# Who makes the high half of the softmax probabilities: one helper's choice of engine

## The chip, the cores and the metric

The kernel runs on one core of one Trainium2 chip. The metric is the device time of one execution in microseconds (us); a comparison of versions goes by the median of several executions. PE is the matrix engine, ACT the scalar engine, DVE the vector engine, POOL is GpSimd, and SP is the engine whose queue issues most of the DMAs.

## The reference

One layer of a hybrid encoder on a sequence of 2048 positions with 1024 features, in float32. Cut to what matters here:

```python
u    = rms_norm(h, norm1_w)
proj = einsum('bsd,de->bse', u, w_in)            # dq | dk | dv | sq | sk | sv
# differential attention: 4 heads, two softmax maps per head, value width 128
logits = einsum('bqhcd,bkhcd->bhcqk', qb, k) * scale + bias   # dq, dk are normed before
logits = where(mask, logits, -inf)               # chunk-causal, chunks of 64
p      = softmax(logits, axis=-1)
attn   = p[:, :, 0] - lam * p[:, :, 1]           # the probabilities of this case
y_diff = einsum('bhqk,bkhd->bqhd', attn, v)
# stick-breaking attention: 8 heads of width 64, no softmax, strictly causal
h = h + concat(norm(y_diff), norm(y_sb)) @ w_out
h = h + SwiGLU(rms_norm(h))                      # width 2816
```

## The kernel before

All large products run on PE in float16 with each operand split in two: a high part (the value cast to float16) and a low part (the value minus its high part, cast to float16). Three products (high by high, high by low, low by high) then stand for one in float32. So each tile of attention probabilities has to be split before PE can use it.

**Stages.** The input projection is cut into eight groups `g`. Groups 0 to 3 hold one softmax head each (function `diff_attn`), groups 4 to 7 two stick-breaking heads each (`sb_attn`). The loop at the end of the first phase goes through the groups; while the heads of group g are worked on, the generator `proj_stream` gives out the projection tiles of the next group, so the two kinds of work share all engines. The output projection and the feed-forward stage follow.

**A softmax head** goes over 16 blocks `i` of 128 queries. `probs(i)` makes the scores of both maps on PE, brings them into tiles `z` with their maxima on DVE (lines 542 and 546), takes the exponentials on ACT in place (line 556), and joins the two maps into one on DVE: `z0 = z1 * rc + z0` (line 566, both inputs in SBUF). Block i reaches over (i+1)*128 keys, in tiles of at most 1024: one tile for i below 8, two from there on. That gives 96 tiles in the four heads, 40 of them with 1024 elements in each partition. Each goes through `split_t` (line 449): a cast into the front of a buffer `s16` by `to16`, a subtraction into its back by `tt` (line 98), and a DMA transpose issued by SP (line 460) into a tile `aT`. There are three `s16` buffers. `values(i)` multiplies `aT` with the values `v` on PE (line 517, in `pv`); it is called two blocks behind `probs`. The tiles' names in the profile are cut: `s` stands for `s16`.

**The choice of engine.** `to16` and `tt` ask `pick` for an engine: the one with the least running sum after its own cost. The sums (`load`) are kept while the program is written, not on the chip; `note` adds work that has a fixed engine; `level` sets them to zero at every fourth block.

```python
def to16(dst, src, n, engines="ADP", psum=False):
    cost = {"A": 0.84 * n + 110, "D": (1.05 if psum else 0.53) * n + 70, "P": 1.1 * n + 80}
    e = pick(**{k: cost[k] for k in engines})
# tt: cost = {"D": 1.15 * n + 70, "P": 2.45 * n + 80}, engines="DP"
def split_t(src, n, he="ADP", le="DP", wide=None):
    ...
    to16(s16[:, :n], src, n, he)
    tt(s16[:, n : 2 * n], src, s16[:, :n], ALU.subtract, n, le)
    ...
    SP.dma_start_transpose(aT[:, : 2 * n // P, :], s16[:, : 2 * n])
```

`to16` writes a cast as an ACT copy (line 89), a DVE copy (line 91) or a POOL instruction (line 93). The stick-breaking heads call `split_t` with ACT for the cast and POOL for the subtraction already.

The same two helpers serve the batches of queries and keys of the groups below 4 (`proj_batch`, line 386, once for every four projection tiles): one multiplication of `raw` by `gk` with `tt` (line 402), then twice a cast of 512 elements from `raw` into `st` (line 406) and its subtraction (line 407). ACT also empties the projection's PSUM tiles `pj` (lines 360 and 374); there are two of them.

**The order** of the instructions on each engine is set by the framework's scheduler, which simulates the program; within an engine they start in that order. The attention work has a raised priority.

Of the kernel before, what the change touches and what calls it, by code (L numbers as in the profile page):

```python
# [59 lines left out]
def block(tc, a, out):  # L60
# [3 lines left out]
    with top:  # L64
# [8 lines left out]
        def note(e, ns):  # L73
            load[e] += ns * KW[e]
# [10 lines left out]
# [3 lines that stand above are left out]
            if e == "A":  # L88
                ACT.copy(dst, src)  # L89
            elif e == "D":  # L90
                DVE.tensor_copy(dst, src)
            else:
                POOL.tensor_scalar(dst, src, 1.0, 0.0, op0=ALU.mult, op1=ALU.add)

        def tt(dst, a_, b_, op, n, engines="DP"):
            cost = {"D": 1.15 * n + 70, "P": 2.45 * n + 80}
            e = pick(**{k: cost[k] for k in engines})
            (DVE if e == "D" else POOL).tensor_tensor(dst, a_, b_, op)  # L98

        def pri(k):  # L100
            def deco(f):
                @functools.wraps(f)
                def g(*args):
                    with tc.high_priority(PRI[k]) if PRI[k] else nullcontext():
                        return f(*args)
                return g
            return deco

        def nm(s):
            uid[0] += 1  # L110
            return f"{s}{uid[0]}"
# [144 lines left out]
        with ExitStack() as ph1:  # L256
# [6 lines left out]
            def z4():  # L263
                return zp.tile([P, 1028], F32, tag="z4", bufs=ZB, name=nm("z4"))
# [183 lines left out]
            @pri("spl")  # L448
            def split_t(src, n, he="ADP", le="DP", wide=None):
                if wide is not None and wide % 5 in (1, 3):  # L450
                    s16 = pp.tile([P, 4, 256], F32, tag="raw", name=nm("s16"))[:].rearrange("p t n -> p (t n)").bitcast(F16)
                else:
                    s16 = s16p.tile([P, 2048], F16, tag="s16", bufs=SB, name=nm("s16"))
                to16(s16[:, :n], src, n, he)
                tt(s16[:, n : 2 * n], src, s16[:, :n], ALU.subtract, n, le)
                if wide is not None and wide % 4 == 3:
                    aT = pp.tile([P, 4, 4, 2, 64], F16, tag="st", name=nm("aT"))[:].rearrange("p c t s e -> p (c t) (s e)")
                else:
                    aT = sp.tile([P, 16, P], F16, tag="aT", bufs=AB, name=nm("aT"))
                SP.dma_start_transpose(aT[:, : 2 * n // P, :], s16[:, : 2 * n])  # L460
                return aT
# [40 lines left out]
            @pri("sc")  # L502
            def score_chunk(G, sc, i, q, m, w, cut=False, turned=False):
                terms = ((m, 0), (2 + m, 0), (m, 1)) if turned else ((2 + m, m), (m, m))
                for o, (a_, b_) in enumerate(terms):
                    last = PE.matmul(sc[:, : 128 * w].rearrange("p (t n) -> p t n", n=P), lhsT=G["q"][i // 4][:, a_, i % 4, :], rhs=G["k"][q][:, b_, 0:w, :], start=o == 0, stop=o == len(terms) - 1)  # L506
                if cut:
                    last = PE.matmul(sc[:, 128 * w - P : 128 * w], lhsT=idb[:], rhs=tri[:], start=False, stop=True, skip_group_check=True)
                return last.ins
# [9 lines left out]
            def diff_attn(g, G):  # L519
                @pri("at")  # L520
                def probs(i):
                    L = (i + 1) * 128
                    near = max(0, i - 1) * 128
                    nb = i // 8 + 1
                    zs = [[], []]
                    if i % 4 == 0:
                        sums[0] = sm.tile([P, 4, 2], F32, tag="sums", bufs=3, name=nm("sums"))
                    su = sums[0][:, i % 4, :]
                    mx = sm.tile([P, 2, 8], F32, tag="mx", name=nm("mx"))
                    for m in range(2):  # L530
                        nx = 0
                        for b in range(nb):
                            n = min(1024, L - 1024 * b)
                            z = z4()
                            for c in range((n + 511) // 512):
                                lo, hi = 512 * c, min(512 * c + 512, n)
                                sc = ps.tile([P, 512], F32, tag="sc", bufs=4, name=nm("sc"))
                                score_chunk(G, sc, i, 2 * b + c, m, (hi - lo) // P)
                                f = min(max(near - 1024 * b - lo, 0), hi - lo)
                                note("D", 1.05 * (hi - lo) + 200)  # L540
                                if f > 0:
                                    DVE.tensor_scalar(z[:, lo : lo + f], sc[:, :f], kz_d[:], None, op0=ALU.mult, op1=ALU.max, accum_out=mx[:, m, nx : nx + 1])
                                    nx += 1
                                if f < hi - lo:
                                    b0 = 1024 * b + lo + f - (i - 1) * 128
                                    DVE.tensor_tensor_reduce(z[:, lo + f : hi], sc[:, f : hi - lo], bias[:, g, b0 : b0 + hi - lo - f], kz_d[:], -3.0e38, ALU.add, ALU.max, mx[:, m, nx : nx + 1])
                                    nx += 1
                            zs[m].append((b, n, z))
                    ng = sm.tile([P, 2], F32, tag="ng", name=nm("ng"))
                    if nx > 1:  # L550
                        DVE.tensor_reduce(ng[:], mx[:, :, :nx], op=ALU.max, axis=AX.X)
                    ACT.activation(ng[:], ng[:] if nx > 1 else mx[:, :, 0], AF.Identity, bias=lnc[:], scale=-1.0)
                    s2 = sm.tile([P, 2, 2], F32, tag="s2", name=nm("s2")) if nb > 1 else None
                    for m in range(2):
                        for b, n, z in zs[m]:
                            ACT.activation(z[:, :n], z[:, :n], AF.Exp, bias=ng[:, m : m + 1], accum_out=(s2[:, m, b : b + 1] if nb > 1 else su[:, m : m + 1]))
                            note("A", 0.84 * n + 300)
                    if nb > 1:
                        DVE.tensor_reduce(su, s2[:], op=ALU.add, axis=AX.X)
                    rc = sm.tile([P, 1], F32, tag="rc", name=nm("rc"))  # L560
                    DVE.reciprocal(rc[:], su[:, 1:2])
                    DVE.tensor_scalar(rc[:], rc[:], mlam[:], su[:, 0:1], op0=ALU.mult, op1=ALU.mult)
                    note("D", 600)
                    aTs = []
                    for (b, n, z0), (_, _, z1) in zip(*zs):
                        DVE.scalar_tensor_tensor(z0[:, :n], z1[:, :n], rc[:], z0[:, :n], op0=ALU.mult, op1=ALU.add)
                        note("D", 1.05 * n + 130)
                        aTs.append((b, n, split_t(z0[:, :n], n)))
                    return aTs

                sums = {}
# [13 lines left out]
                for i in range(NT):  # L585
                    if i % 4 == 0:
                        level()
                    held.append((i, probs(i), sums[0]))
                    if len(held) > 2:
                        values(*held.pop(0))  # L590
                    yield ((i + 1) * (i + 2) / 2 + CD * (i + 1)) / (136 + 16 * CD), i + 1
# [706 lines left out]
```

## Time and profile before

| What | us |
|---|---|
| median of three executions | 2706.24 (2704.32 to 2712.25) |
| the profiled execution | 2704.82 |
| its span, first to last instruction | 2702.7 |
| PE busy in the span | 2500.8 |
| DVE busy | 1956.5 |
| POOL busy | 1516.4 |
| ACT busy | 1346.4 |

The span is what the views of the profile divide up; the time of the execution is 2.1 us more. Busy time is the sum of an engine's instructions; the waits are listed apart, each with the instruction that ended it.

### The profile page before, as it was taken

The page shows a single profiled execution, that of the slowest core. Times are in us where ns is not written, and L with a number is a line of the kernel's source. Part 1 is how long each engine was busy: PE and PEld are TensorE (multiplying, and loading weights), DVE is VectorE, ACT ScalarE, POOL GpSimd, SP SyncE. Part 2 cuts the span into 40 slices and gives each one's busy share as a digit, 9 for nine tenths or more (in the row PEclk, how much of TensorE's full clock was granted, in tenths as well). Part 3 has the DMA queues.
Part 4 walks back from the last instruction along what each step waited for, and adds up shares of the span by engine and source line. Part 5 has one row for each costly group of instructions (what it writes and reads, how often), then busy time and mean ns, then how long its engine had stood idle before and what let it go on. Part 6 is the DMA issues. An engine that isn't in the chain of part 4 may idle for free. (4 is left out here: it accounts for less than half of the span.)

```text
span 2702.7 us, 50511 instructions
## 1 busy us (share of the span) xinstructions
PE 2500.8 (93%) x19628; PEld 1502.5 (56%) x19628; DVE 1956.5 (72%) x3711; ACT 1346.4 (50%) x2488; POOL 1516.4 (56%) x1097
## 2 busy tenths in 40 slices
PE   7998989898988989889998999999999999999999
PEld 4655556577776776567784444444444444444444
DVE  6888879899989989877856777778685543433434
ACT  4665656567978878665735534345352112111121
POOL 2577767767767767546655565565564332322322
PEclk9999999999999999999999999999999999999999
DMA  7777687769989989987995566565749744635532
GB/s 230 201 166 180 143 200 173 178 151 178 196 176 185 178 169 209 206 200 211 222 335 204 210 236 220 198 234 190 253 171 338 293 158 160 234 132 184 201 111 94
DMA packets 619584, 534.40 MB, mean 198 GB/s; under 512 B 480640, under 2 KB 548224, under 8 KB 609104
## 3 DMA queue, kind: packets, MB, share of 16 engines
q1 hardware_dynamic: 617520, 529.09, 69.8%
q8 instruction: 154, 2.52, 0.4%
q0 software_dynamic: 512, 1.36, 0.2%
q10 hardware_dynamic: 1312, 0.72, 0.1%
q14 instruction: 86, 0.70, 0.1%
HBM read 261.08 MB, written 147.32 MB: 151 GB/s over the span
## 5 line engine op out<-in xcount | busy, mean ns | idle before, releaser
L98 POOL TENSOR_TENSOR s<-z,s 128x1024 f16<-128x1024 f32 (+7 forms) x288 | 471.9, 1648 | 140.9 <-ACT s L89 116.3
L506 PE MATMUL sc<-kT,qT 128*128 128x512 f16 (+3 forms) x1520 | 381.6, 353 | 53.5 <-DVE z L622 19.0
L1104 PE MATMUL pd<-wd,act 128*128 128x512 f16 x1764 | 391.8, 379 | 8.1 <-DVE cu L1038 7.1
L621 DVE TENSOR_TENSOR_SCAN z<-z,sc 128x512 f32<-128x512 f32 (+3 forms) x320 | 352.8, 1112 | 56.7 <-ACT sc L619 34.9
L325 PE MATMUL pj<-w,xt 128*128 128x384 f16 x1920 | 353.1, 332 | 17.2 <-ACT raw L374 5.9
L1004 PEld LDWEIGHTS <-wg 128*128 128x128 f16 x1848 | 181.5, 98 | 226.1 <-issue 12.4
L1004 PEld LDWEIGHTS <-wu 128*128 128x128 f16 x1848 | 181.5, 98 | 220.2 <-issue 7.1
L517 PE MATMUL yp<-v,aT 128*128 128x64 f16 (+1 forms) x4896 | 269.1, 204 | 37.3 <-DMA aT<-s 36.2
L517 PEld LDWEIGHTS <-aT 128*128 128x128 f16 x4896 | 236.9, 99 | 115.4 <-DMA aT<-s 47.7
L98 POOL TENSOR_TENSOR act<-cg,act 128x512 f16<-128x512 f32 x109 | 150.6, 1392 | 262.5 <-ACT act L1063 262.5
L1104 PEld LDWEIGHTS <-act 128*128 128x128 f16 x1764 | 172.6, 98 | 216.6 <-issue 10.1
L325 PEld LDWEIGHTS <-xt 128*128 128x128 f16 x1920 | 187.5, 99 | 146.9 <-issue 23.3
L89 ACT CAST s<-z 128x128 f16<-128x128 f32 (+7 forms) x215 | 173.1, 810 | 135.8 <-DMA aT<-s 41.0
L98 POOL TENSOR_TENSOR stages<-stages 128x512 f32<-128x512 f32 x97 | 171.6, 1769 | 119.1 <-DVE wg L220 41.3
L618 ACT ACTIVATE z<-sc,c 128x512 f32<-128x512 f32 (+3 forms) x320 | 210.6, 663 | 25.1 <-PE sc L506 12.5
L98 POOL TENSOR_TENSOR hs<-hs,cu 128x512 f32<-128x512 f32 x102 | 132.5, 1307 | 158.1 <-DVE hs L1110 58.0
L506 PEld LDWEIGHTS <-qT 128*128 128x128 f16 x1520 | 128.2, 99 | 121.4 <-issue 23.5
L1063 ACT CAST act<-cg 128x512 f16<-128x512 f32 x126 | 76.8, 616 | 237.5 <-DVE cg L1069 199.4
L831 PE MATMUL po<-wo,mt 128*128 128x256 f16 x1536 | 182.5, 279 | 12.2 <-DVE xf L834 8.4
L1110 DVE SCALAR_TENSOR_TENSOR hs<-pd,c,hs 128x512 f32<-128x512 f32 x144 | 106.5, 748 | 116.3 <-PE pd L1104 112.2
L341 PE MATMUL pj<-xt,w 128*128 128x128 f16 x2304 | 176.9, 222 | 6.2 <-DVE v L363 5.2
L1004 PE MATMUL pm<-X,wu 128*128 128x512 f16 x792 | 179.3, 379 | 1.8 <-ACT cg L1049 1.7
(255 smaller groups left out, 4803.5 us busy)
## 6 DMA issues: line engine op xcount, KB each, us to landing
xt<-xs SPq DMA_DIRECT2D x112, 512.0 KB, 4.3
hs<-hd SPq DMA_DIRECT2D x72, 512.0 KB, 4.4
hd<-hs SPq DMA_DIRECT2D x56, 512.0 KB, 5.4
split<-wg SPq DMA_DIRECT2D x11, 1792.0 KB, 6.9
split<-wu SPq DMA_DIRECT2D x11, 1792.0 KB, 6.7
split<-wd SPq DMA_DIRECT2D x11, 1792.0 KB, 6.8
wg<-split SPq DMA_DIRECT2D x11, 1792.0 KB, 7.3
wd<-split SPq DMA_DIRECT2D x11, 1792.0 KB, 8.7
```

What stands on the lines that cost most here:

```text
L89: ACT.copy(dst, src)
L98: (DVE if e == "D" else POOL).tensor_tensor(dst, a_, b_, op)
L325: PE.matmul(pj[:, :384], lhsT=xv[:, xi, kt, :], rhs=G["w"][:, wi, kt, :], start=n == 0, stop=n == 23)
L341: PE.matmul(o, lhsT=x_ if c == 2 else w_, rhs=w_ if c == 2 else x_, start=n == 0, stop=n == 23)
L506: last = PE.matmul(sc[:, : 128 * w].rearrange("p (t n) -> p t n", n=P), lhsT=G["q"][i // 4][:, a_, i % 4, :], rhs=G["k"][q][:, b_, 0:w, :] ...
L517: PE.matmul(yp[:, y0 : y0 + wd], lhsT=aT[:, a_, :], rhs=v[:, v_ : v_ + wd], start=start and j == 0 and q == 0, stop=stop and j == nb - 1 a ...
L618: ACT.activation(om[:, lo:hi], sc[:, :w], AF.Sigmoid, scale=G["nkz"][:])
L621: DVE.tensor_tensor_scan(ov, ov, sc[:, :w], om[:, hi : hi + 1], op0=ALU.mult, op1=ALU.bypass)
L831: PE.matmul(po[:, sl], lhsT=mt[:, kt, P * xi : P * xi + P], rhs=wos[2 * h + n][wi][:, kt, :], start=q == 0, stop=q == 23)
L1004: PE.matmul(ps_[:].rearrange("p (t n) -> p t n", n=P), lhsT=wv[:, wo, wi, 128 * kt : 128 * kt + 128], rhs=X[xo][:, :, xi, kt, :], start=st ...
L1104: PE.matmul(po[:], lhsT=act[:, ao, xi, 128 * j : 128 * j + 128], rhs=W["d"][:, wo, wi, :], start=start and u == 0 and q == 0, stop=u == nu ...
L1110: DVE.scalar_tensor_tensor(dst, po[:], kd[:], src, op0=ALU.mult, op1=ALU.add)
```

## The change

In `diff_attn` the call of `split_t` gets "A" as its third argument, so that the cast of the probabilities is always an ACT instruction. The subtraction is chosen as before among DVE and POOL. The costs still enter the running sums.

```diff
@@ -565,7 +565,7 @@
                     for (b, n, z0), (_, _, z1) in zip(*zs):
                         DVE.scalar_tensor_tensor(z0[:, :n], z1[:, :n], rc[:], z0[:, :n], op0=ALU.mult, op1=ALU.add)
                         note("D", 1.05 * n + 130)
-                        aTs.append((b, n, split_t(z0[:, :n], n)))
+                        aTs.append((b, n, split_t(z0[:, :n], n, "A")))
                     return aTs
```

## The prediction

> **What bounds the kernel now.** I read the page first, then the busy time by window, then the waits of PE, then the groups of the stage that the change touches.
>
> ```profile
> span 2702.7 us, 50511 instructions
> PE 2500.8 (93%) x19628; PEld 1502.5 (56%) x19628; DVE 1956.5 (72%) x3711; ACT 1346.4 (50%) x2488; POOL 1516.4 (56%) x1097
> 110.00:615.00 505.00, 458.18 (x4029) 308.31 (x4028) 440.25 (x1306) 311.08 (x801) 360.28 (x257) 0.98 0.74 170
> ```
>
> The last row is the window from 110 to 615 us, in which the 96 tiles of the softmax heads are joined (line 566). Its columns after the length are the busy times of PE, weight loads, DVE, ACT and POOL. PE is busy 458.2 of 505 us, DVE 440.3, POOL 360.3, ACT 311.1. So PE stands still for 46.8 us; that is all that any change of this stage can win there, 1.7% of the span. What PE waits for in the same window:
>
> ```profile
> PE yp L517 <- DMA aT<-s: 23.5, 16, 2.9
> PE pj L325 <- ACT raw L374: 5.9, 3, 3.4
> PE sc L506 <- DVE z L542: 3.7, 7, 1.5
> ```
>
> Columns: total us, number, longest. Half of PE's idle time is the wait for transposed probabilities, which is the end of the chain join (566), cast, subtraction, transpose. The cast is a link of this chain. The second row matters for the price: ACT also empties the projection's PSUM tiles, and PE stops when it is late with that.
>
> **The part that moves.** The groups of this window, by line:
>
> ```profile
> L98 POOL TENSOR_TENSOR s<-z,s 128x1024 f16<-128x1024 f32 (+6 forms) x95 | 160.0, 1694 | 12.8 <-ACT s L89 9.9
> L93 POOL TENSOR_SCALAR s<-z 128x1024 f16<-128x1024 f32 (+7 forms) x72 | 78.8, 1099 | 95.3 <-DVE z L566 93.6 <-DMA aT<-s 1.8
> L89 ACT CAST st<-raw 128x512 f16<-128x512 f32 x27 | 16.6, 614 | 27.0 <-POOL raw L98 12.7 <-DVE raw L399 12.2 <-DVE ng L551 2.0
> L89 ACT CAST s<-z 128x128 f16<-128x128 f32 (+6 forms) x24 | 15.3, 636 | 34.6 <-DMA aT<-s 16.6 <-DVE z L566 12.0 <-DVE mx L546 3.7
> ...
> L93 POOL TENSOR_SCALAR s<-z x73: 301/1047/2014, 111.3 to 617.3; 128x1024 f16<-128x1024 f32 x37, 128x640 f16<-128x640 f32 x8, 128x384 f16<-128x384 f32 x7, 128x896 f16<-128x896 f32 x5
> L93 POOL TENSOR_SCALAR st<-raw x1: 617/617/617, 68.1 to 68.1; 128x512 f16<-128x512 f32 x1
> ```
>
> Of the 96 casts POOL does 73 and ACT 23 (the 24th ACT cast of the window is of a stick-breaking head); DVE does none. All subtractions are on POOL. The change therefore moves 73 casts from POOL to ACT. Their price on each side:
>
> ```profile
> L93 POOL TENSOR_SCALAR s<-z 128x1024 f16<-128x1024 f32 x37 | 50.6, 1368 | 66.3 <-DVE z L566 66.3
> L89 ACT CAST s<-z 128x1024 f16<-128x1024 f32 x3 | 3.1, 1045 | 5.5 <-DVE z L566 5.5
> L89 ACT CAST s<-z 128x512 f16<-128x512 f32 x4 | 2.5, 614 | 11.1 <-DMA aT<-s 11.1
> ```
>
> *POOL loses* 78.8 us of work, and with it the 93.6 us that it stood waiting for the join in front of these casts. *ACT gains* 37 times 1.045 us, 38.7 us, and the 36 smaller ones: the two ACT rows give 0.842 ns an element and 0.183 us for each instruction; 8 of 640, 7 of 384, 5 of 896 and 16 others (four each of 768, 512, 256 and 128, what is left of the eight tiles of each size) are 18,944 elements, so 16.0 + 6.6 = 22.6 us. Together 61.3 us.
>
> *A second move hides in the running sums.* Every cast that goes to ACT raises ACT's sum and leaves POOL's lower, and the next choice reads these sums. Followed through the listing, they give for the program before 23 ACT and 73 POOL casts, as the trace has. At the third query/key batch of a group, for example, they stand at ACT 11,374 and POOL 13,789 before (POOL already with the multiplication by `gk`), so the 512-element cast goes to ACT (11,374 + 540 against 13,789 + 643). With the change they are 14,609 and 9,808, and it goes to POOL. This turns round in all 12 batches of groups 1 to 3: 24 casts `st<-raw` go from ACT to POOL, at 0.617 us by the one such row of POOL, 14.8 us. All subtractions stay on POOL, and all evictions of `pj` stay on ACT, since DVE's sum is the largest throughout.
>
> Net in the window: ACT 311.1 + 61.3 - 14.7 (24 times 0.614) = 357.7 of 505 us, 71%; POOL 360.3 - 78.8 + 14.8 = 296.3 us, 59%. Neither becomes the fullest engine. None of this is on the path by itself; what counts is whether `aT` comes sooner and what ACT delays.
>
> **What the chain gains: an ordinary block.** From the timeline, block 12 of the third head, with two tiles:
>
> ```profile
> 453.04 2.35 DVE L566 SCALAR_TENSOR_TENSOR z<-z,rc,z 128x1024 f32<-128x1024 f32 x2
> 454.57 1.13 ACT L556 ACTIVATE z<-z,ng 128x1024 f32<-128x1024 f32 x1
> 454.68 2.30 POOL L93 TENSOR_SCALAR s<-z 128x1024 f16<-128x1024 f32 x2 [1.17 <-DVE z L566]
> 455.71 0.92 ACT L556 ACTIVATE z<-z,ng 128x768 f32<-128x768 f32 x1
> 456.95 3.48 POOL L98 TENSOR_TENSOR s<-z,s 128x1024 f16<-128x1024 f32 x2
> 459.11 2.89 SPq L460 DMA_TRANSPOSE aT<-s  x2
> 459.87 2.58 DVE L566 SCALAR_TENSOR_TENSOR z<-z,rc,z 128x1024 f32<-128x1024 f32 x2
> ```
>
> POOL does both casts (2.30 us), then both subtractions. On ACT the first cast would end at 454.68 + 1.05 = 455.73, and POOL could start its subtraction then instead of at 456.95: 1.2 us sooner. But at 454.68 ACT is in the exponentials of the next block, which end at 456.63. If the scheduler puts the cast behind them, it ends at 457.68, 0.7 us later than now. So one block lies between 1.2 us gained and 0.7 us lost. I take 0.5 us gained, nearer to the gain, since ACT is free for 38% of the window even before anything is relieved.
>
> The 1024-element cast took 1.368 us on POOL, beside DVE's second join, and 1.045 us on ACT: 37 x 0.32 = 12 us that POOL loses beside DVE and ACT does not. I count them as POOL's time only, as they stand in the 78.8 us already. The Trainium skill, "SBUF — State Buffer", section "Who interferes with whom", has a rule for this: DVE and GpSimd share a pair of ports, an instruction of DVE with two SBUF inputs takes it against a GpSimd instruction that reads SBUF, the second to come waits in full, and ACT never waits. The trace agrees with the part on ACT; were the joins as often the blocked side, DVE would get up to the same 12 us back by that rule, which would be the last rival below.
>
> **What the chain gains: the change of heads.** At 350 to 375 us (and likewise near 220 and 490) POOL is behind:
>
> ```profile
> 358.25 1.64 POOL L93 TENSOR_SCALAR s<-z 128x128 f16<-128x128 f32 x2
> 359.88 3.50 POOL L219 TENSOR_SCALAR w<-wst,sW 128x1536 f16<-128x1536 f32 x2
> 363.35 2.00 POOL L93 TENSOR_SCALAR s<-z 128x384 f16<-128x384 f32 x1
> 365.32 2.55 POOL L98 TENSOR_TENSOR s<-z,s 128x128 f16<-128x128 f32 x2
> 367.27 2.48 SPq L460 DMA_TRANSPOSE aT<-s  x2
> 369.12 0.62 ACT L89 CAST st<-raw 128x512 f16<-128x512 f32 x1 [6.37 <-POOL raw L98]
> 369.60 0.34 PE L517 MATMUL yp<-v,aT 128*128 128x128 f16 x3 [2.67 <-DMA aT<-s]
> ```
>
> Casts of 1.64 and 2.00 us stand in POOL's queue ahead of the subtractions for which PE then waits 2.67 us, while ACT stands idle for 6.37 us behind a cast of `raw` that needs POOL. With the change the 3.6 us leave POOL's queue, and the cast that held ACT goes to POOL. Here I take the whole wait away: 2.67 us, at three changes of heads some 5 us beyond the ordinary 0.5 each (between 0, if the order there is unkind, and 8).
>
> **Sum.** Sixteen waits for `aT`: 16 x 0.5 = 8 us, less than the 23.5 they have; the changes of heads bring it to 13 at best. Against it: 61 us more ACT work, of which some delays an eviction. The row is 5.9 us of PE waiting for ACT in 505 us; in proportion to ACT's idle time (193.9 us before, 147.3 after) it would be 7.8, so 2 us, and the same again for the exponentials that come later and so the joins of the next block: 4 us. A PE that waits less for `aT` also meets the next late thing, scores whose `z` DVE has not yet emptied (3.7 us now, 440 of 505 us of DVE work); I give back 4 of the 13 to that. 13 - 4 - 4 = 5 us. The profiled execution, 2704.82 us, becomes 2699.8; the median of the runs lies 1.4 us above it, so I predict 2701 us, between 2688 (waits gone) and 2705. A measurement of this kernel can tell about 0.3%, 8.1 us, from no change.
>
> **The rivals.**
>
> *ACT is held up in order (slower).* A cast can't start before its `s16` buffer is free, that is before a transpose has landed. On POOL such a wait holds only other casts and subtractions. On ACT it holds the exponentials and the evictions.
>
> ```profile
> 236.33 9.52 SPq L460 DMA_TRANSPOSE aT<-s  x4
> 243.43 0.45 POOL L93 TENSOR_SCALAR s<-z 128x256 f16<-128x256 f32 x1 [1.08 <-DMA aT<-s]
> 245.34 0.51 POOL L93 TENSOR_SCALAR s<-z 128x384 f16<-128x384 f32 x1 [0.70 <-DMA aT<-s]
> ```
>
> At the change of heads the transposes went out from 236.33 in 9.52 us, and POOL's next casts waited for them. ACT's 24 casts already wait 16.6 us for `aT`, 0.69 us each, and 34.6 us in all. With 72 more at 1.44 us, ACT stands 104 us longer, of the 147 that it has left. It decides once ACT waits for a buffer while both `pj` tiles are full; three changes of heads at half of the 9.52 us each (two `pj` tiles cover the other half), 14 us, and the 16 waits for `aT` at the 0.7 us lost above, 11 us, less the 8 us that the rest still gains, make 17 us: 2723. For it speaks the 16.6 us; against it that the joins follow each other on DVE (453.04 and 459.87 above, 6.8 us apart), and in between ACT has nothing to take up but what DVE gives it, so that such a wait often costs nothing.
>
> *Nothing comes of it.* PE and DVE are the full engines and neither loses an instruction; if the time freed before `aT` turns into waits for scores, the sum is 0 to 2 us: 2705. By the Trainium skill, "Perfetto Trace Analysis", section "Identifying the Most-Contended Engine", one works on the engine with the highest occupancy first, which is neither POOL nor ACT. By that rule alone the result would be this one; the trace is half with it, for 23.3 of PE's 46.8 idle us aren't waits for `aT`.
>
> *It wins more.* All 23.5 us of waits go, and only 4 come back: 2685 to 2688. It needs the cast ahead of the exponentials in nearly every block.
>
> That the change does not do what it says I leave at nothing: the argument is passed on as it stands.
>
> **How the numbers follow.** Small gain, 0.40; held up in order, 0.30; nothing, 0.15; more, 0.15. Faster by over 8.1 us: the last case, and nearly half of the first (its range to 2688 passes 2698), 0.15 + 0.19 = 0.34. Slower: the second case, 0.30. Within: the rest, 0.36. The range reaches from the large gain to past the middle of the slow case, 2684 to 2728.
>
> **What would show it.** Right: in the window ACT near 358 us and POOL near 296 of some 500; 24 casts `st<-raw` at line 93; the subtraction's row with ACT as what ended its waits; PE's wait for `aT` under 16 us; ACT's wait for POOL's `raw` gone. Wrong to the slow side: "PE pj L325 <- ACT raw L374" above 15 us, "ACT s L89 <- DMA aT<-s" above 60. Wrong altogether: a changed time behind 615 us, where no instruction is another one and only the order could have moved.

## The result and the profile after

The changed kernel is slower, by little but clear of the noise: 2724.57 us median of 6 runs (2719.45 to 2731.82), the kernel before 2708.12 (2703.47 to 2712.25) beside it. The ratio is 1.0058 [1.0041, 1.0074], about 16 us. The forecast was 2701; to a clearly slower kernel it gave a chance of 0.30. The profiled execution took 2725.54 us, its span 2723.4.

The page after, its first lines, and the window of the softmax stage (columns after the length: PE, weight loads, DVE, ACT, POOL, granted clock, DMA share, GB/s):

```profile
span 2723.4 us, 50531 instructions
PE 2509.9 (92%) x19628; PEld 1509.5 (55%) x19628; DVE 1971.7 (72%) x3711; ACT 1387.3 (51%) x2537; POOL 1462.9 (54%) x1048
110.00:615.00 505.00, 457.22 (x3956) 304.34 (x3955) 447.53 (x1303) 343.75 (x838) 308.08 (x207) 0.98 0.76 169
```

In the same 505 us PE issued 3956 matmuls where it had issued 4029. The groups and waits of the stage (110 to 620 us, since the last join now starts at 618.7):

```profile
L98 POOL TENSOR_TENSOR s<-z,s 128x1024 f16<-128x1024 f32 (+4 forms) x93 | 162.3, 1756 | 140.3 <-ACT s L89 139.3 <-POOL s L98 0.8
L566 DVE SCALAR_TENSOR_TENSOR z<-z,rc,z 128x1024 f32<-128x1024 f32 (+4 forms) x96 | 129.9, 1382 | 0.9
L89 ACT CAST s<-z 128x1024 f16<-128x1024 f32 (+4 forms) x94 | 72.3, 785 | 50.4 <-DVE z L566 17.6 <-DMA aT<-s 12.7 <-issue 7.7
L93 POOL TENSOR_SCALAR st<-raw 128x512 f16<-128x512 f32 x24 | 19.5, 825 | 0.0
L89 ACT CAST st<-raw 128x512 f16<-128x512 f32 x4 | 2.4, 610 | 1.2 <-DVE raw L399 1.2
```

The joins before:

```profile
L566 DVE SCALAR_TENSOR_TENSOR z<-z,rc,z 128x1024 f32<-128x1024 f32 (+4 forms) x96 | 111.4, 1188 | 0.8
```

The waits after that bear on the argument, then the second of them before:

```profile
PE yp L517 <- DMA aT<-s: 18.7, 16, 2.9
PE sc L506 <- DVE mx L546: 10.7, 14, 3.4
DVE z L542 <- POOL s L98: 7.7, 3, 5.8
PE pj L325 <- ACT raw L374: 3.3, 4, 1.5
```
```profile
PE sc L506 <- DVE mx L546: 3.7, 4, 2.8
```

The moved work is where it was said to be: POOL's subtractions now wait for ACT (139.3 us), POOL makes 24 casts of `raw`. PE waits 4.8 us less for `aT` and 7.0 us more for DVE's `mx` (3.7 before). The joins take 129.9 us, 111.4 before.

The second part of the loss comes behind this stage. The window that follows it, first of before, then of after:

```profile
615.00:860.00 245.00, 218.16 (x3379) 175.25 (x3376) 223.93 (x395) 203.49 (x382) 181.85 (x139) 0.99 0.95 184
```
```profile
615.00:860.00 245.00, 209.60 (x3177) 172.14 (x3175) 214.10 (x376) 197.02 (x371) 174.42 (x132) 0.95 0.87 176
```

Only the end of the softmax stage (its last cast ends at 622 us) still holds moved casts there, yet PE does 202 matmuls less, and the granted clock, the share of full speed at which PE may run, is 0.95 where it was 0.99. A part of the matmuls is missing only because PE comes to them later; the table of shifts further down takes that out. How one such place begins, in the timeline of after:

```profile
617.47 4.34 DVE L566 SCALAR_TENSOR_TENSOR z<-z,rc,z 128x1024 f32<-128x1024 f32 x2
617.80 5.75 POOL L98 TENSOR_TENSOR s<-z,s 128x1024 f16<-128x1024 f32 x2 [14.71 <-ACT s L89]
...
622.12 0.39 DVE L363 SCALAR_TENSOR_TENSOR v<-pj,v 128x256 f16<-128x256 f32 x1
...
622.57 0.72 PE L341 MATMUL pj<-w,xt 128*128 128x128 f16 x6 [4.89 <-DVE v L363]
```

The last two joins run beside two subtractions of POOL and take 4.34 us (the pairs of the prediction took 2.35 and 2.58); the eviction of `v` stands behind them on DVE, and PE waits 4.89 us for it. Then the clock falls: in the 14 us from 617 to 631 it is 0.88, where before it was 1.00 (one stretch of 3.4 us at half speed, from 622.7).

```profile
617.00:631.00 14.00, 9.11 (x112) 7.78 (x109) 12.52 (x24) 12.26 (x25) 11.34 (x7) 0.88 0.60 133
```

Over the whole run the clock records show half speed for 116.1 us, 88.7 before, in stretches of 3.4 us and multiples of it. The Trainium skill, "TensorE: Matmul & The Clock Gate", section "Part 1: The HAM clock gate", says that the clock halves after an idle window of about 3.4 us and returns after a busy one. The lengths agree with that. A wholly idle window was not needed here: in the 3.4 us ahead of the stretches PE was busy for up to 46% before and up to 52% after.

So there were two questions: what do the moved casts cost, and what does the new order cost that the scheduler draws once the program is another one? Compared by line, tiles and shape, 1422 of DVE's 3711 instructions and 4984 of PE's 19628 matmuls stand at another place of their engine's sequence than before, from early in the softmax stage on.

### The profile page after: what moved, and what is told of

It reads as the page before. It is cut to its first block, busy times and chain, and to the rows that moved or that the text cites. A ratio compares the mean times of both kernels' runs of the same rounds, so it can differ in the third digit from the quotient of the medians.

```text
span 2723.4 us, 50531 instructions
## 1 busy us (share of the span) xinstructions
PE 2509.9 (92%) x19628; PEld 1509.5 (55%) x19628; DVE 1971.7 (72%) x3711; ACT 1387.3 (51%) x2537; POOL 1462.9 (54%) x1048
## 3 DMA queue, kind: packets, MB, share of 16 engines
q0 software_dynamic: 512, 1.36, 0.1%
## 5 line engine op out<-in xcount | busy, mean ns | idle before, releaser
L98 POOL TENSOR_TENSOR s<-z,s 128x1024 f16<-128x1024 f32 (+7 forms) x288 | 477.4, 1666 | 280.4 <-ACT s L89 251.7
L89 ACT CAST s<-z 128x1024 f16<-128x1024 f32 (+7 forms) x288 | 232.6, 815 | 154.9 <-DMA aT<-s 36.0
L618 ACT ACTIVATE z<-sc,c 128x512 f32<-128x512 f32 (+3 forms) x320 | 209.5, 660 | 41.5 <-PE sc L506 22.1
L341 PE MATMUL pj<-xt,w 128*128 128x128 f16 x2304 | 183.8, 226 | 15.6 <-DVE v L363 12.3
L1004 PE MATMUL pm<-X,wg 128*128 128x512 f16 x792 | 181.3, 382 | 1.9 <-ACT bx L1179 1.9
```

The lines of the kernel that those rows point to most:

```text
L341: PE.matmul(o, lhsT=x_ if c == 2 else w_, rhs=w_ if c == 2 else x_, start=n == 0, stop=n == 23)
L618: ACT.activation(om[:, lo:hi], sc[:, :w], AF.Sigmoid, scale=G["nkz"][:])
L1004: PE.matmul(ps_[:].rearrange("p (t n) -> p t n", n=P), lhsT=wv[:, wo, wi, 128 * kt : 128 * kt + 128], rhs=X[xo][:, :, xi, kt, :], start=st ...
```

## The experiments

The theories: **A**, the casts on ACT stand behind the exponentials, so subtractions start later and get in the way of DVE's joins; **B**, POOL's longer chain for queries and keys (the 24 casts of `raw`) costs; **C**, it is the order that the scheduler draws, whatever the edit.

**Each half alone, and two neutral edits, order left to the scheduler.** `on=` forces an engine after `pick` has kept its sums, so that nothing else turns round.

```diff
-            e = pick(**{k: cost[k] for k in engines})
+            e = pick(**{k: cost[k] for k in engines}); e = on or e
 # e1: only the sums' second move
+ to16(d[:, :, :, 0, :], src, 512, on="P" if g > 0 else None)
 # e2: only the 73 casts
+ split_t(z0[:, :n], n, "ADP", "DP", None, "A")
 # e5: one cast, head 0, block 2;  e6: one cast, head 2, block 5
+ split_t(z0[:, :n], n, "ADP", "DP", None, "A" if (g, i) == (0, 2) else None)
```

Only the `raw` casts:

> The running sums are those of the program before; only the 24 casts from raw into st of groups 1 to 3 are moved from ACT to POOL, as the change did on its side. Theory A (the probabilities' casts stand in ACT's order behind the next block's exponentials, so POOL's subtractions start later and block DVE's joins): nothing, 2705 to 2711 us, joins (L566) in all 114 us as before. Theory B (POOL's longer chain to queries and keys is what costs): most of the loss, 2716 to 2724, PE waiting for qT over 5 us. Theory C (it is the order that the scheduler draws after any small edit, not the cast's engine): anything between 2695 and 2725, without relation to what was moved.

Only the 73 casts:

> The running sums are those of the program before; all 96 casts of the probabilities are on ACT, and the casts into st stay on ACT too. Theory A: all of the loss, 2718 to 2730 us, joins over 128 us in all. Theory B: none or little, 2705 to 2712. Theory C: anything between 2695 and 2725.

One cast of 384 elements:

> A control: one single cast of 384 elements (block 2 of the first head) goes to ACT instead of POOL, the sums untouched. By its own cost it is worth under 1 us. Theories A and B: 2706 to 2710 us. Theory C: the scheduler orders all that follows anew, and the time moves by up to 15 us either way.

One cast of 768 elements:

> A second control: one single cast of 768 elements (block 5 of the third head) goes to ACT, the sums untouched. Theories A and B: 2706 to 2710 us. Theory C: up to 15 us either way, and not the same as in the first control.

| Edit | us | ratio |
|---|---|---|
| 24 casts of `raw` to POOL | 2732.59 | 1.0092 [1.0077, 1.0107] |
| 73 casts to ACT | 2733.55 | 1.0095 [1.0082, 1.0108] |
| one cast of 0.5 us to ACT | 2744.04 | 1.0126 [1.0113, 1.0140] |
| another single cast | 2717.92 | 1.0037 [1.0024, 1.0050] |

One cast of half a microsecond costs 36 us. Each half costs more than the whole. Three of the four times lie above every range that was written down, C's too. Nothing about A or B can be read from such runs; C is the only theory that fits a single cast of this price, and the order has to be taken out of the comparison.

**The order held.** The program is built twice. The first build, with the engines of before, gives the scheduler's order; in the second, order edges tie each engine's instructions to that order, whoever now makes the casts. (A cast that has changed engine stands where it stood among all instructions.) Then the engines are the only difference.

```diff
+    held = plain_order(inputs)               # first build: names, order
     with tile.TileContext(nc, schedule_with_timeline_sim=True) as tc:
-        block(tc, aps, o[0])
+        block(tc, aps, o[0], True)
+        hold_order(tc, held)                 # each after the one before it on its engine
 # on= "A" for: h5 (g, i) == (0, 2) | h1 all | h2 all, and "P" for raw | h4 i >= 8 | h3 i < 8
 #              h9 i >= 8 and b == 0 (first tiles) | h10 i >= 8 and b > 0 (second tiles)
```

One cast:

> The same single cast as in the first control, but with every engine's order held as the scheduler made it for the program before: only this one instruction changes its engine, and stands in ACT's queue where it stood in the common order of issue. Theory C (the order that the scheduler draws is what costs): 2706 to 2710 us, all of the control's 36 us gone. If the cast itself mattered: 2735 and more.

All 73:

> All 73 casts from POOL to ACT, each at its place in the common order of issue, all other instructions of all engines in the order of before. Theory A (late casts on ACT, subtractions that block joins): 2718 to 2730 us, joins over 128 us. Theory C: 2700 to 2712, and the casts' own effect on the time is what is left, the first forecast's small gain (2700 to 2705) or a few us of loss.

The whole change:

> The whole change with the order held: 73 casts of the probabilities from POOL to ACT and 24 casts into st from ACT to POOL. Theory A: as the run before it or worse, 2718 to 2732. Theory B (POOL's longer chain to queries and keys): 5 us or more above the run with the casts alone. Theory C: 2700 to 2714.

Blocks 8 to 15:

> Order held; only the casts of blocks 8 to 15 go to ACT (41 of the 73), those of blocks 0 to 7 stay on POOL. After the change the chain from join to end of subtraction is longer in these late blocks and shorter in the early ones. Theory A: the whole loss sits here, 2716 or more, and above the run with all casts moved. Theory C: within 4 us of the run with all casts moved.

Blocks 0 to 7:

> Each engine's order is held as it was drawn for the kernel before; only the casts of the probabilities of blocks 0 to 7 (one tile a block, 32 of the 73) go from POOL to ACT. If the loss comes from ACT standing in order behind the exponentials of the late blocks, this costs little: 2708 to 2713 us, and PE's wait for aT in the softmax stage stays within 2 us of the 23.9 of before. If the costs of early and late blocks add up to those of all 73 casts (2726.7, late alone 2722.1), it is about 2713. If the early blocks gain (after their joins the subtraction ends 3 us sooner in the changed kernel), it falls under 2705.

First tiles of blocks 8 to 15:

> Order held; only the casts of the first tile (1024 elements) of blocks 8 to 15 go to ACT. That cast is the one that the prediction's block 12 priced: between 1.2 us gained and 0.7 lost. If the loss is the cast that stands behind the exponentials of the next block, so that POOL's subtractions and z come later, this kernel has most of the 14 us that all late casts cost: 2716 to 2722. If the first cast is rather a gain because POOL can subtract sooner, it is 2700 to 2708.

Second tiles:

> Order held; only the casts of the second tile (128 to 1024 elements) of blocks 8 to 15 go to ACT, the first stays where it was. On POOL the second cast stands in front of the first subtraction; without it that subtraction starts sooner, but the second subtraction then waits for ACT. If the loss comes from late second tiles (in the changed kernel their subtraction ended 1.7 us later behind the join, that of the first tile 0.9 us later), this has most of the 14 us: 2716 to 2722; if from the first ones, 2706 to 2712.

| Casts moved to ACT, order of before held | us | ratio |
|---|---|---|
| one (the same that cost 36 us) | 2708.87 | 1.0001 [0.9988, 1.0014] |
| all 73 | 2726.69 | 1.0064 [1.0051, 1.0076] |
| all 73, and 24 of `raw` to POOL | 2727.91 | 1.0067 [1.0055, 1.0079] |
| 41 of blocks 8 to 15 | 2722.08 | 1.0054 [1.0039, 1.0068] |
| 32 of blocks 0 to 7 | 2713.00 | 1.0014 [1.0005, 1.0023] |
| the 32 first tiles of blocks 8 to 15 | 2724.12 | 1.0058 [1.0041, 1.0074] |
| 9 second tiles of blocks 8 to 15 (the other 23 were on ACT before) | 2705.86 | 0.9990 [0.9979, 1.0002] |

Each time stands against the kernel before in the same series (2708.36 for the first four rows, 2709.48 for the last three). The 36 us of the single cast were all order. With that gone the parts add up: early 3.5 and late 14 us make the 18 of all 73, B is within the noise (1.2 us), and the late part is the **first tiles** alone. (All 32 of them were on POOL before; the 30 and 28 in two expectations below are miscounts.) The waits from 110 to 632 us that bear on this, first tiles on ACT, then second tiles on ACT, then before:

```profile
PE yp L517 <- DMA aT<-s: 30.9, 22, 4.2
ACT s L89 <- DVE z L566: 29.7, 14, 4.1
DVE z L546 <- POOL s L98: 11.3, 3, 4.8
ACT s L89 <- DMA aT<-s: 9.6, 8, 2.7
DVE z L542 <- POOL s L98: 7.3, 5, 2.4
PE pj L325 <- ACT raw L374: 5.6, 3, 2.5
```
```profile
PE yp L517 <- DMA aT<-s: 25.3, 19, 3.8
ACT s L89 <- DMA aT<-s: 21.3, 7, 3.9
ACT s L89 <- DVE z L566: 7.8, 4, 3.1
DVE z L546 <- POOL s L98: 4.0, 3, 2.3
DVE z L542 <- POOL s L98: 0.3, 1, 0.3
```
```profile
PE yp L517 <- DMA aT<-s: 23.9, 17, 2.9
DVE z L546 <- POOL s L98: 4.0, 3, 2.3
DVE z L542 <- POOL s L98: 1.0, 3, 0.5
```

With the first tiles moved, DVE waits 18.6 us for POOL to have read a `z` tile (4.3 in the other kernel, 5.0 before), and PE waits longer for `aT`. The evictions of `pj` are no part of it, and of theory A's second half, joins in POOL's way, little is left: with all 73 casts moved the 96 joins took 114.6 us, 111.4 before, where A had named over 128. Block 14 of the third head, lines from the timeline of before and of the kernel with the first tiles on ACT:

```profile
471.74 2.34 DVE L566 SCALAR_TENSOR_TENSOR z<-z,rc,z 128x1024 f32<-128x1024 f32 x2
473.10 1.88 POOL L93 TENSOR_SCALAR s<-z 128x1024 f16<-128x1024 f32 x1 [4.91 <-DVE z L566]
475.06 2.14 POOL L98 TENSOR_TENSOR s<-z,s 128x1024 f16<-128x1024 f32 x1
477.24 0.48 DVE L546 CUSTOM_DVE_ANT_0 z<-sc,bias,c 128x256 f32<-128x256 f32 x1 [0.91 <-POOL s L98]
```
```profile
480.04 2.34 DVE L566 SCALAR_TENSOR_TENSOR z<-z,rc,z 128x1024 f32<-128x1024 f32 x2
480.57 1.15 ACT L556 ACTIVATE z<-z,ng 128x1024 f32<-128x1024 f32 x1
...
483.98 1.14 ACT L556 ACTIVATE z<-z,ng 128x1024 f32<-128x1024 f32 x1
485.12 1.87 ACT L89 CAST s<-z 128x1024 f16<-128x1024 f32 x2
486.22 2.13 POOL L98 TENSOR_TENSOR s<-z,s 128x1024 f16<-128x1024 f32 x1 [10.86 <-ACT s L89]
488.38 0.48 DVE L546 CUSTOM_DVE_ANT_0 z<-sc,bias,c 128x256 f32<-128x256 f32 x1 [3.75 <-POOL s L98]
488.93 0.61 PE L506 MATMUL sc<-kT,qT 128*128 128x512 f16 x2 [0.67 <-DVE mx L546]
```

POOL began its cast 1.36 us after the start of the joins. ACT begins it 5.08 us after: four exponentials of the next block stand ahead of it, two maps of two tiles. The subtraction ends 2.8 us later; DVE, which has to write new scores into the `z` tile that the subtraction reads, stands 3.75 us instead of 0.91; and PE waits for the scores' `mx` behind that. Followed tile by tile, the subtraction of 17 of the 32 first tiles ends later behind its join, by 0.3 to 3.3 us and 26.2 in sum; that of the other 15 sooner, by 0.2 to 1.1 and 11.4 in sum.

**Only the casts that came sooner.** Is it the place in ACT's order, or ACT itself?

```diff
 # h11: second tiles, and 13 first tiles whose cast had ended sooner on ACT
+ "A" if MOVE and i >= 8 and (b > 0 or (g, i) in SOONER) else None
```

> Order held; to ACT go all casts of second tiles (as in the kernel that moves only those, 2705.9 us) and 13 casts of first tiles, those that ended sooner behind their join on ACT than on POOL in the trace where all first tiles were moved (there 0.1 to 4.0 us sooner; the others 0.9 to 4.0 us later, behind the next block's exponentials). If what costs is the cast's place behind the exponentials and nothing else, this kernel costs nothing: 2700 to 2707. If any first cast on ACT costs by its engine alone, 13 of 30 of the 14.6 us of all first casts come on top of 2705.9: about 2712.

It took 2708.34 us, 0.9995 [0.9983, 1.0007] (2710.45 before in this series). Of its waits, 110 to 632 us:

```profile
ACT s L89 <- DVE z L566: 26.3, 13, 3.1
PE yp L517 <- DMA aT<-s: 22.1, 16, 3.9
...
DVE z L546 <- POOL s L98: 4.0, 3, 2.3
```

ACT still stands 26.3 us in wait for the joins, and it costs nothing; what is gone is DVE's wait for POOL. So the loss belongs to the other 19 first casts, those that end later on ACT, and a first cast costs through its place behind the exponentials. Nor does the sooner end win anything that can be measured: PE's wait for `aT` is 22.1 us beside the 23.9 of before.

**The changed kernel's own order.** The same holding, turned round: the order of the changed kernel, with the engines of before (k1), or with the changed engines but for the late first tiles (k2).

```diff
 # k1: first build with the whole change, second without
-        block(tc, aps, o[0])                 # in plain_order
+        block(tc, aps, o[0], True)
 # k2: second build with "A" only if i < 8 or b > 0
```

The new order alone (k1):

> Each engine's order is held as it was drawn for the changed kernel; the engines of all casts are those of the kernel before. If the new order is what costs in the changed kernel, it stays near 2724 us (2718 to 2735). If the moved casts cost there too what they cost in the old order, 18 to 20 us, it falls to 2704 to 2708; then the scheduler's new order would be as good as the old one, and only the casts are to blame. Above 2735: the new order was drawn for casts on ACT and fits casts on POOL still less; then in that order the move is a gain.

Without the late first tiles (k2):

> The changed kernel's order and its engines, but the casts of the first tiles of blocks 8 to 15 are on POOL (28 of them) as before. If first tiles cost here as they do in the old order, 12 to 16 us below the changed kernel: 2708 to 2713. If the scheduler, which knew that these casts were ACT's, placed them so that they cost nothing, it is the changed kernel's 2724.6 within 4 us or more than that.

k1 took 2716.53 us, 1.0036 [1.0022, 1.0049]; k2 2720.24, 1.0049 [1.0035, 1.0062]. Both lie between the cases that had been written down. In the table the start of the last join (612.9 us in the trace of before), of the first scan of the stick-breaking heads (line 621, at 602) and of the 121st (at 848), each as its shift against before in one profiled execution (the kernel with one cast moved in the held order, which costs nothing, shows +2.0, +2.0 and +1.6):

| Order | Engines | ratio | last join | first scan | 121st scan |
|---|---|---|---|---|---|
| before | changed (h2) | 1.0067 | +21.1 | +18.6 | +20.5 |
| after | before (k1) | 1.0036 | -1.9 | -1.1 | +14.3 |
| after | changed, late first tiles not (k2) | 1.0049 | +2.1 | +2.9 | +15.1 |
| after | changed | 1.0058 | +5.8 | +8.5 | +18.6 |

In its own order the change costs in the softmax stage 7.7 to 9.6 us instead of 18 to 21: the order that was drawn with these casts on ACT carries them better. The late first tiles have 3.7 to 5.6 us of that (after against k2), where they cost 14.6 in the old order; by the times alone these two kernels aren't apart. The stage by itself is as short in the new order as in the old one. The price is behind it: 10 to 15 us between the first and the 121st scan, with either set of engines. Between these two scans the clock records show half speed for 6.8 us before, 5.5 in h2, 41.0 in k1, 27.7 in k2 and 23.9 after. Counted as half a microsecond lost for each one at half speed, an estimate, that is 17.1, 10.4 and 8.5 us more than before in the last three, beside 15.4, 12.2 and 10.1 us that they lose there. So by its size the lost clock can be most of the price; no run separates it from the gaps of PE that go with it. k1's row of that window has still less clock than that of after, with PE busy 215.46 us for 3197 matmuls:

```profile
615.00:860.00 245.00, 215.46 (x3197) 176.47 (x3195) 209.94 (x370) 190.33 (x358) 170.22 (x131) 0.92 0.88 175
```

By the times alone, order and casts of the changed kernel aren't apart (the intervals of 1.0036 and 1.0058 overlap); the shifts by place are what separates them. Other places for the first casts in ACT's held order, or a fourth `s16` buffer, were not tried.

## Why the prediction was wrong

*The choice of engines* was right to the instruction: 96 casts on ACT, 24 casts of `raw` on POOL, no subtraction elsewhere. *Busy times:* ACT 343.8 us for the 357.7 forecast, POOL 308.1 for 296.3. The window holds 2% fewer matmuls, so probably less of ACT's work; and the casts of `raw` took 0.825 us on POOL, not the 0.617 of the one row shown, 5 us in 24. The 93.6 us for which POOL stood waiting in front of its casts did not go with them: POOL now waits in front of the subtractions (139.3 us for ACT).

*The ordinary block* is the step that failed. "So one block lies between 1.2 us gained and 0.7 us lost. I take 0.5 us gained, nearer to the gain, since ACT is free for 38% of the window." Block 12, from which the bounds came, was in fact 0.79 us later with the first tiles moved. But it is no ordinary block. Its row shows two exponentials behind the join; where all four stand ahead, as in block 14, it is 2.8 us, and 3.3 in the worst block. Nor is the gain that of most blocks: in block 12 POOL makes both casts ahead of its first subtraction, but 23 of the 32 second tiles were on ACT already. In such a block, as in 14, POOL's subtraction stands behind one cast of POOL (1.88 us there, on ACT 1.03), and a cast that began at the same moment on ACT would win 0.85 us, not 1.2. ACT's idle share says nothing about that moment: in blocks 12 and 14 the next block's exponentials begin within 0.6 us of the join. And the two ends don't weigh the same: a subtraction that comes sooner has little waiting for it, one that comes later holds `z`, DVE and then PE. So 8 us of gain stood where the held order has 14 us of loss and the changed kernel's own order 4 to 6.

*The change of heads* was right in part. With the order held and all casts moved, the wait of 2.67 us is gone, two smaller ones of 1.35 and 0.22 us stand a little earlier, and from the last join of a head to the first of the next head's block 8 the shift of the joins falls by 1.6, 0.7 and 0.9 us at the three changes, some 3 us for the 5 forecast. But at the first change PE's longest wait rose from 2.48 to 4.11 us, and the early blocks of the first head, which follow no other head, bring a shift of 4.6; the early blocks as a whole lost 3.5.

*What ACT delays:* 4 us were set down for evictions and later exponentials. The evictions cost nothing in the changed kernel (3.3 us after, 5.9 before); with all casts moved in the held order they took 7.3 us, near the 7.8 of the forecast. *Given back:* 4 us were allowed for scores not yet emptied; PE's wait for scores with `z` not yet emptied was 2.8 us after (3.7 before), that for `mx` grew by 7.0, but it is 10.5 in k1 too, so that is the new order.

*The rival "held up in order"* gave 2723, and its kind, a cast in order on ACT, is what the held runs show. That its time came within 2 us of the measured one is luck: its 14 us were for buffers at the changes of heads, and about half of the loss is the order's. Its two signs did not come: ACT's wait for a buffer fell to 12.7 us (23.0 with all casts moved and the order held, where above 60 was named), and no `pj` tile was late. The hold-up is not ACT's, it is POOL's and DVE's behind ACT. *"Nothing"* fails in either order.

*The order* had no term in the sum at all, only a last sentence: "a changed time behind 615 us, where no instruction is another one and only the order could have moved". That is where 10 us of the changed kernel's loss arise (15 in k1). So this is the second step that failed: a term that the sum put at nothing. Five new orders were drawn here, by changes large and tiny; all five kernels came out slower, by 10 to 36 us (in two of them and in the changed kernel the moved casts have a part). A chance for that belonged into the forecast before any block was priced.

*Open:* why the new order costs what it does between 615 and 860 us. Seen are gaps of PE and the half clock after them. Between the first and the 121st scan before has no gap of over 2 us, the changed kernel six, of 2.8 to 4.9 us; k1, with the casts of before, has six at the same instructions. Four of the six end with DVE's eviction of `v` (line 363). So these gaps belong to the order and not to the moved casts. Which instruction's new place makes them was not tried, nor why the order of before is better than all five others.

## What to carry to other kernels

Where a scheduler sets the order, even a tiny edit can draw much of it anew: run a neutral edit first to see how much that alone moves, and hold the order to learn what an engine's work is worth. Before work goes to an engine with idle time, look at what stands on it at the moment when the input becomes ready, in every kind of block and not in one; here four exponentials stood there. Price the two ends apart: an operation that comes later may hold a buffer which the fullest engine needs, and one that comes sooner may win nothing.

## What the runs showed of the hardware

The joins with 1024 elements took 1.54 us in the mean before and 1.70 after, though DVE's instructions are the same:

```profile
L566 DVE SCALAR_TENSOR_TENSOR z<-z,rc,z 128x1024 f32<-128x1024 f32 x40 | 61.2, 1538 | 0.6
```
```profile
L566 DVE SCALAR_TENSOR_TENSOR z<-z,rc,z 128x1024 f32<-128x1024 f32 x40 | 67.7, 1699 | 0.7
```

More of them ran beside a subtraction of POOL, as the pair of 4.34 us above: 55 of the 96 after, 32 before. Against the shortest join of the same size, all 96 lost 22.7 us before and 41.3 after; those beside a subtraction had 18.2 and 40.5 of it. The 23 joins of before that ran beside a cast of POOL and nothing else of POOL lost 0.2 us together; there the cast was longer, 1.37 us where ACT took 1.05. So the prediction's casts are relieved by the move, but it was the subtractions, 2.1 us each, that the joins lost time to. How many of them meet is mostly set by the order: the joins take 123.6 us in k1, with the casts on POOL, and 114.6 with all casts on ACT in the old order. And a gap of PE costs twice: the one of 4.89 us was followed by 3.4 us at half the clock.
